# A four-layer forward pass on one core: norm and residual in turn on DVE, latent products operand by operand, decays by ACT's bias

## The chip, the cores and the metric

One core of a Trainium2 chip runs the whole program. TensorE (PE) multiplies into PSUM, VectorE (DVE), ScalarE (ACT) and GpSimd (POOL) do the rest, and SyncE (SP) and ACT issue DMAs. The metric is device time of one execution in microseconds (us), the median of three runs.

## What is computed

The input is 1024 tokens of 1024 numbers, float32. Three layers follow each other, retention with gated output, latent attention (MLA) and gated linear attention (GLA), then a feed-forward network with squared ReLU and a last norm (the reference also defines forgetting attention, which its depth of one leaves out). The parts that matter here, cut from the reference:

```python
def rmsnorm(x, g):
    y = xf * lax.rsqrt(jnp.mean(xf * xf, axis=-1, keepdims=True) + RMS_EPS)
    return (y * g.astype(jnp.float32)).astype(x.dtype)
# end of the retention layer and of the MLA layer
return x + rmsnorm(y, g_post)
# start of the second layer
a = rmsnorm(h, g_kv) @ w_kv_a              # latent keys and values, 256 + 64 wide
proj = rmsnorm(h, g_pre) @ w_in            # latent queries, 384 wide, and the gate
# GLA, one chunk: b is the running sum of the log decays
k_dec = kb * jnp.exp(b_last - b)
decay = jnp.exp(jnp.where(causal, b_i - b_j, -jnp.inf))
```

## The kernel before

Activations lie transposed: eight tiles (k = 0 to 7) of 128 features by 512 tokens for each half h of the tokens. Each operand of a product is split in a high part (ACT copies) and a low part (DVE subtracts), and each product takes three matmuls (`mm3`, lines 227 to 232). Weights are split likewise (`load_parts`, line 128): SP loads them, POOL scales them by a gain where there is one (L135), ACT writes the high part (L143), DVE the low part (L144); two raw buffers, four slots for the parts. PSUM has eight banks in three pools; `acc_tile` hands out five of them in turn.

Norms: `Norm.add` squares a tile on ACT and adds it up on the engines of its list in turn (L265); `rstd` sums over partitions on PE (L273), makes mean plus epsilon on DVE (`var`, L309) and the power on POOL (L312); `spread` brings the result to all partitions by PE (L320) and ACT (L328). `Next` takes each finished tile of a layer: it squares it, stores it, splits it into operands (L187, L188) and, some due units later, emits the norm (`rows`). `tick` counts these units down as products are emitted. `Later` counts them down on demand, when something asks for a value that has not been emitted yet.

First hand-over. `a_last` (L1062) does the last quarter of the first layer's output product for both halves and adds it to y (L1085). After each half, `finish(h)` (L1144) multiplies all y tiles by gain and norm on DVE (L1152), adds the layer's input `xres` (L1161, tile 0 on DVE, the others on POOL) and gives the tile to `nb`, whose norm alternates between DVE and POOL. Then `gemm_group` (L348) makes the latent products in groups of three weights: queries (h = 0), keys and values (h = 0), queries (h = 1), keys and values (h = 1). Each product runs through all eight operands before the next begins, and the three are evacuated at the end with the new norm (`raw`, L1221, `rope`, L334 to L340). The gate products follow.

Second hand-over. `b_out` (L1517) makes the second layer's output product in four parts (`ps_out`), adds them (L1546), and defers `finished` (L765), which multiplies by gain and norm (L778) and adds the layer's input (L782, on DVE for the tiles in `B_ADDS`, on POOL otherwise). `each` is the third layer's `NextC`: its `Blocks` split the tiles and make seven sums of blocks for a multiplication scheme with seven products per 2 by 2 blocks (L193, L454, L463). The first three weight jobs (`job_of_c`, L1852) begin on the first blocks; their weights' low parts are on POOL.

Levels. In the third layer `c_levels` (L1687) makes the masked decays of one head and half, eight times: the decayed key `kd` (POOL subtracts, ACT exponentiates L1706, POOL multiplies L1707, PE transposes L1772), and seven levels of blocks of width L = 64 to 1: `decayed` subtracts a reference column on DVE (L1725), takes the magnitude and the exponential on ACT (L1726, L1727), and multiplies on DVE (L1730). It runs as a side generator between the layer's products.

The order on each engine is not the program's: a planner places every instruction by priority and by times from its own model of the machine, when the program is built. `high_priority` and `urgent` raise a step. On the chip each engine then runs its list in order, and an instruction that waits holds up all behind it.

## Time and profile before

| | us |
|---|---|
| median of 3 runs | 2600.33 |
| lowest, highest | 2598.05, 2600.61 |
| the profiled execution | 2598.72 |
| its span, first to last instruction | 2596.7 |
| PE busy in it | 2448.0 |
| DVE busy | 2001.0 |
| POOL busy | 1184.9 |
| ACT busy | 1114.1 |

The span is what the trace covers; 2.0 us of the execution lie around it. Times in the trace count from the span's start. L12 is line 12 of the kernel. A releaser in brackets is what ended an engine's idle time. A granted clock of 1.00 is 2.4 GHz, 0.50 is 1.2 GHz. In a time line an instruction's length holds some overlap with the next one, so the pitch between starts is the cost of one in a row.

### The profile page before, as it was taken

The page shows a single profiled execution, that of the slowest core. Times are in us where ns is not written, and L with a number is a line of the kernel's source. Part 1 is how long each engine was busy: PE and PEld are TensorE (multiplying, and loading weights), DVE is VectorE, ACT ScalarE, POOL GpSimd, SP SyncE. Part 2 cuts the span into 40 slices and gives each one's busy share as a digit, 9 for nine tenths or more (in the row PEclk, how much of TensorE's full clock was granted, in tenths as well). Part 3 has the DMA queues.
Part 4 walks back from the last instruction along what each step waited for, and adds up shares of the span by engine and source line. Part 5 has one row for each costly group of instructions (what it writes and reads, how often), then busy time and mean ns, then how long its engine had stood idle before and what let it go on. Part 6 is the DMA issues. An engine that isn't in the chain of part 4 may idle for free.

```text
span 2596.7 us, 35526 instructions
## 1 busy us (share of the span) xinstructions
PE 2448.0 (94%) x12676; PEld 2049.2 (79%) x12676; DVE 2001.0 (77%) x2939; ACT 1114.1 (43%) x1932; POOL 1184.9 (46%) x873
## 2 busy tenths in 40 slices
PE   7999999999998899999998998899999999999998
PEld 5888888878786688888887787877777888788877
DVE  8787686789987853766659768895788777867786
ACT  7323323254443333555544354444453333543334
POOL 4344454534754831322206344554546666433355
PEclk8999999999998899999999899999999999999999
DMA  6523223534333322122234242456424344644432
GB/s 230 158 84 122 102 82 121 207 98 126 108 116 98 122 87 78 51 67 78 86 116 142 79 134 102 155 174 207 134 106 154 138 155 152 236 141 140 142 130 90
DMA packets 153101, 327.62 MB, mean 126 GB/s; under 512 B 17467, under 2 KB 20923, under 8 KB 152924
## 3 DMA queue, kind: packets, MB, share of 16 engines
q1 hardware_dynamic: 131036, 285.49, 33.6%
q10 hardware_dynamic: 21888, 39.86, 4.0%
q8 instruction: 100, 1.64, 0.3%
q14 instruction: 77, 0.63, 0.1%
HBM read 224.09 MB, written 99.09 MB: 124 GB/s over the span
## 4 chain that ended last, share of the span: by engine, by line
PE 64%; DVE 20%; issue 5%; DMA 4%; POOL 3%; ACT 3%; SPq 0%; ACTq 0%; DVEq 0%; POOLq 0%
PE ps L230 13%; PE ps L232 13%; PE ps L231 13%; DVE wl L630 3%; DVE swap L840 2%; PE ps L522 2%; PE ps L521 2%; PE ps L523 1%; DVE z L1730 1%; PE ps_g L230 1%; PE ps_g L232 1%; PE ps_g L231 1%; PE pt L1453 1%; DVE y L550 1%; PE ps_out L230 1%
## 5 line engine op out<-in xcount | busy, mean ns | idle before, releaser
L629 ACT ACTIVATE wh<-ws 128x1024 fp32r<-128x1024 f32 (+3 forms) x200 | 142.7, 725 | 193.3 <-PE ps L231 109.4
L630 DVE TENSOR_TENSOR wl<-ws,wh 128x1024 fp32r<-128x1024 f32 (+3 forms) x196 | 205.0, 1053 | 20.1 <-ACT wh L629 19.6
L638 POOL TENSOR_TENSOR wsb<-wsc 128x512 f32<-128x512 f32 (+2 forms) x72 | 102.7, 1426 | 254.2 <-issue 173.2
L230 PE MATMUL ps<-hi,wh 128*128 128x512 f32 (+1 forms) x488 | 185.9, 382 | 2.5 <-DVE y L2174 1.7
L232 PE MATMUL ps<-hi,wl 128*128 128x512 f32 (+1 forms) x488 | 184.0, 382 | 3.9 <-DVE wl L630 3.0
L231 PE MATMUL ps<-lo,wh 128*128 128x512 f32 (+1 forms) x488 | 185.4, 380 | 0.0
L629 ACT ACTIVATE wh<-wsb 128x1024 fp32r<-128x1024 f32 (+2 forms) x76 | 73.6, 968 | 222.1 <-PE ps L231 165.1
L638 POOL TENSOR_TENSOR ws<-ws,wsb 128x512 f32<-128x512 f32 (+2 forms) x72 | 99.1, 1377 | 116.9 <-DVE wl L630 116.9
L1428 POOL TENSOR_SCALAR p<-p,rl 128x512 f32<-128x512 f32 (+2 forms) x96 | 61.0, 646 | 195.8 <-DVE rl L1426 94.0
L638 POOL TENSOR_TENSOR wsb<-ws,wsb 128x512 f32<-128x512 f32 (+2 forms) x72 | 114.0, 1583 | 75.5 <-DMA ws<-w_a 40.9
L550 DVE TENSOR_TENSOR y<-ps,y 128x512 f32<-128x512 f32 x112 | 76.6, 684 | 75.5 <-PE ps L232 45.0
L550 DVE TENSOR_TENSOR one<-ps,one 128x512 f32<-128x512 f32 x168 | 113.9, 681 | 19.4 <-PE ps L232 17.3
L550 DVE TENSOR_TENSOR y<-ps,one 128x512 f32<-128x512 f32 x108 | 73.5, 685 | 64.0 <-ACT one L556 23.0
L630 DVE TENSOR_TENSOR wl<-wsc,wh 128x1024 fp32r<-128x1024 f32 (+2 forms) x76 | 108.0, 1425 | 11.2 <-ACT wh L629 10.6
L232 PEld LDWEIGHTS ps<-hi,wl 128*128 128x128 f32 x488 | 91.7, 188 | 25.6 <-DVE wl L630 5.2
L638 POOL TENSOR_TENSOR wsc<-wsc,ws 128x512 f32<-128x512 f32 (+2 forms) x72 | 110.9, 1540 | 0.0
L230 PEld LDWEIGHTS ps<-hi,wh 128*128 128x128 f32 x488 | 91.7, 188 | 23.3 <-DVE y L2174 2.3
L2174 DVE TENSOR_TENSOR y<-ps,y 128x512 f32<-128x512 f32 x124 | 83.3, 681 | 30.3 <-PE ps L232 29.9
L231 PEld LDWEIGHTS ps<-lo,wh 128*128 128x128 f32 x488 | 91.7, 188 | 18.8
L630 DVE TENSOR_TENSOR wl<-wsb,wh 128x1024 fp32r<-128x1024 f32 (+2 forms) x76 | 96.7, 1273 | 12.7 <-ACT wh L629 12.3
L188 DVE TENSOR_TENSOR lo<-lo,hi 128x512 fp32r<-128x512 f32 x106 | 78.3, 767 | 25.2 <-ACT hi L187 25.2
L629 ACT ACTIVATE wh<-wsc 128x1024 fp32r<-128x1024 f32 (+2 forms) x76 | 73.2, 968 | 57.2 <-PE ps L231 38.4
(473 smaller groups left out, 8594.5 us busy)
## 6 DMA issues: line engine op xcount, KB each, us to landing
lo<-u SPq DMA_DIRECT2D x98, 256.0 KB, 5.2
ws<-w_ff SPq DMA_DIRECT2D x23, 512.0 KB, 3.7
ws<-w_a SPq DMA_DIRECT2D x21, 512.0 KB, 4.9
u<-y SPq DMA_DIRECT2D x42, 256.0 KB, 2.1
ws<-w_b SPq DMA_DIRECT2D x20, 512.0 KB, 3.4
wsc<-w_a SPq DMA_DIRECT2D x16, 512.0 KB, 4.2
v<-v SPq DMA_DIRECT2D x32, 256.0 KB, 3.2
gate<-g SPq DMA_DIRECT2D x32, 256.0 KB, 3.3
```

The source lines that it names most:

```text
L188: (lo_eng or nc.vector).tensor_tensor(out=lo, in0=src, in1=hi.bitcast(F32), op=ALU.subtract)
L230: nc.tensor.matmul(ps, lh, rh, start=start, stop=False)
L231: nc.tensor.matmul(ps, lh, rl, start=False, stop=False)
L232: nc.tensor.matmul(ps, ll, rh, start=False, stop=stop)
L521: nc.tensor.matmul(o, xh[:, ts], wh[:, c], start=k == 0, stop=False)
L522: nc.tensor.matmul(o, xh[:, ts], wl[:, c], start=False, stop=False)
L550: nc.vector.tensor_tensor(out=o, in0=p, in1=i, op=ALU.add)
L629: nc.scalar.activation(out=hi, in_=raw, func=AF.Copy)
L630: lo_eng.tensor_tensor(out=lo, in0=raw, in1=hi.bitcast(F32), op=ALU.subtract)
L638: eng.tensor_tensor(out=o, in0=x, in1=y, op=op)
L1428: nc.gpsimd.tensor_scalar(out=pr, in0=pr, scalar1=rl, scalar2=0.0, op0=ALU.mult, op1=ALU.add)
L2174: nc.vector.tensor_tensor(out=t, in0=ps, in1=t, op=ALU.add)
```

## The change

At both hand-overs, DVE now does the multiplication and the residual addition of a tile one after the other, through two turn buffers, for all eight tiles; POOL does none of these additions. The residual loads of the first hand-over are issued in `a_last`, after the first of its four weights. The norm sums of `nb` are all on POOL, its due time is 13 instead of 10 units. `gemm_group` runs through the operands in its outer loop: for each of the eight, the three matmuls of all three products, with its ticks in two portions. The order of the groups is queries (h = 0), keys and values (both halves), queries (h = 1), so the key and value weights are loaded once and the query weights twice, nine loads for twelve. In the levels, `kd` is made by four exponentials of 128 columns, each with its reference column as ACT's bias, and a product on DVE; for L = 64 and 32 the magnitude is taken by ACT from b with the reference column as bias, in four pieces of 128 and eight of 64 columns, without the subtraction. The low parts of the first weights of the third layer are on DVE.

```diff
-B_ADDS = ((0, 4), (0, 1, 2, 3))
+LEVEL_ACT = 32
-B_WAIT = 10
+B_WAIT = 13
 def gemm_group(srcs, xs, wide, evac, halves=(0, 1), **kw):
...
-            acc = []
-            for m, w in enumerate(ws):
-                acc.append(acc_tile("ps_grp", wide))
-                gemm_t(acc[m], w, 0, [xs[k, h] for k in range(NK)])
+            acc = [acc_tile("ps_grp", wide) for _ in ws]
+            for k in range(NK):
+                c = slice(k * P, k * P + P)
+                for ps, (wh, wl) in zip(acc, ws):
+                    mm3(ps, wh[:, c], wl[:, c], *xs[k, h], k == 0, k == NK - 1)
+                if k % 4 == 3:
+                    tick(len(ws))
...
 class Next:
-        def __init__(self, name, g=None, wait=TILE_UNITS):
+        def __init__(self, name, g=None, wait=TILE_UNITS, on=(nc.vector, nc.gpsimd)):
...
-                self.norm[h] = Norm(D)
+                self.norm[h] = Norm(D, self.on)
...
 def finished(y, h, norm, post, latest, each, order):
...
-            for k in order:
-                t = y[k, h]
+            turns = [stage("turn") for _ in range(2)]
+            for i, k in enumerate(order):
+                t, u = y[k, h], turns[i % 2]
                 nc.vector.scalar_tensor_tensor(
-                    out=t, in0=t, scalar=gain(post, k), in1=rb, op0=ALU.mult, op1=ALU.mult
+                    out=u, in0=t, scalar=gain(post, k), in1=rb, op0=ALU.mult, op1=ALU.mult
                 )
-                eng = nc.vector if k in on_vector else nc.gpsimd
-                eng.tensor_tensor(out=t, in0=t, in1=old[k], op=ALU.add)
+                nc.vector.tensor_tensor(out=t, in0=u, in1=old[k], op=ALU.add)
...
 def a_last(g, norms):
...
                 for s in range(4):
+                    if s == 1:
+                        for k in range(NK):
+                            xres[k, h] = slots.get("xres")
+                            load(xres[k, h], a["x"][k, h])
...
-        nb = Next("b", wait=B_WAIT)
+        nb = Next("b", wait=B_WAIT, on=(nc.gpsimd,))
         def finish(h):
...
+            turns = [slots.get("turn") for _ in range(2)]
             for k in range(NK):
-                xs = slots.get("xres")
-                load(xs, a["x"][k, h])
+                xs = xres.pop((k, h))
...
-                    out=y[k, h],
+                    out=t,
...
-                eng = nc.gpsimd if k else nc.vector
-                eng.tensor_tensor(out=y[k, h], in0=y[k, h], in1=xs, op=ALU.add)
+                nc.vector.tensor_tensor(out=y[k, h], in0=t, in1=xs, op=ALU.add)
...
-        for h in range(2):
-            for o, evac, g in ((0, lat_q.add, gq), (3, evac_kv, gk)):
-                gemm_group(
...
+        for o, evac, g, hs in (
+            (0, lat_q.add, gq, (0,)), (3, evac_kv, gk, (0, 1)), (0, lat_q.add, gq, (1,))
+        ):
+            srcs = [a["w_b"][o + m] for m in range(3)]
+            gemm_group(srcs, nb.x, True, evac, hs, scale=g, nk=NK)
...
 def c_levels(i, h):
...
-        nc.gpsimd.tensor_tensor(
-            out=chunks(kd),
-            in0=chunks(b)[:, :, P - 1 : P].to_broadcast([P, 4, P]),
-            in1=chunks(b),
-            op=ALU.subtract,
-        )
-        nc.scalar.activation(out=kd, in_=kd, func=AF.Exp)
-        nc.gpsimd.tensor_tensor(out=kd, in0=kd, in1=k, op=ALU.mult)
+        for c in range(4):
+            cs = slice(c * P, (c + 1) * P)
+            nc.scalar.activation(
+                out=kd[:, cs],
+                in_=b[:, cs],
+                func=AF.Exp,
+                scale=-1.0,
+                bias=b[:, cs.stop - 1 : cs.stop],
+            )
+        nc.vector.tensor_tensor(out=kd, in0=kd, in1=k, op=ALU.mult)
...
-            nc.vector.tensor_tensor(out=zv, in0=bv, in1=ref, op=ALU.subtract)
-            nc.scalar.activation(out=z, in_=z, func=AF.Abs)
+            if L >= LEVEL_ACT:
+                for o in range(0, HALF, 2 * L):
+                    nc.scalar.activation(
+                        out=z[:, o : o + 2 * L],
+                        in_=b[:, o : o + 2 * L],
+                        func=AF.Abs,
+                        scale=-1.0,
+                        bias=b[:, o + L - 1 : o + L],
+                    )
+            else:
+                nc.vector.tensor_tensor(out=zv, in0=bv, in1=ref, op=ALU.subtract)
+                nc.scalar.activation(out=z, in_=z, func=AF.Abs)
...
 def job_of_c(n, early=False, bank=bank5):
-            w.first(nc.gpsimd if n < C_BEGIN else nc.vector)
+            w.first()
```

## Rows read from the trace of the kernel before

**Rows 1.** The page, parts 1 and 2: busy time by engine, PE's granted clock in 40 slices.

```profile
PE 2448.0 (94%) x12676; PEld 2049.2 (79%) x12676; DVE 2001.0 (77%) x2939; ACT 1114.1 (43%) x1932; POOL 1184.9 (46%) x873
...
PEclk8999999999998899999999899999999999999999
```

**Rows 2.** Table by stage: from:to, length, busy PE PEld DVE ACT POOL (instructions), clock, DMA share, GB/s.

```profile
812.90:918.50 105.60, 82.63 (x370) 66.18 (x370) 89.84 (x87) 42.26 (x64) 75.73 (x42) 0.87 0.37 122
817.50:831.10 13.60, 8.14 (x16) 4.87 (x16) 13.60 (x16) 7.36 (x13) 5.99 (x4) 0.50 0.67 225
918.50:1016.00 97.50, 97.50 (x436) 78.91 (x436) 38.26 (x48) 25.16 (x38) 14.40 (x8) 1.00 0.27 91
1360.20:1469.00 108.80, 95.61 (x462) 80.41 (x461) 92.48 (x106) 49.07 (x78) 57.83 (x34) 0.87 0.34 111
1435.30:1452.30 17.00, 14.93 (x47) 12.80 (x48) 17.00 (x27) 8.96 (x15) 7.09 (x5) 0.50 0.24 82
1495.00:1755.00 260.00, 232.19 (x1542) 205.74 (x1541) 218.00 (x345) 132.76 (x214) 127.78 (x92) 0.97 0.43 141
```

**Rows 3.** PE's time line: start, length, engine, line, out<-in, [idle before, releaser].

```profile
786.28 0.39 PE L232 MATMUL ps<-uh,wl 128*128 128x512 f32 x1
786.51 0.39 PE L230 MATMUL ps<-uh,wh 128*128 128x512 f32 x1
...
819.19 1.89 PE L230 MATMUL ps_grp<-xh,wh 128*128 128x512 f32 x3 [6.29 <-ACT xh L187]
...
872.14 0.79 PE L230 MATMUL ps_grp<-xh,wh 128*128 128x512 f32 x1 [12.65 <-DVE raw L1221]
```

**Rows 4.** DVE's and POOL's time lines, the first layer's end, first half.

```profile
805.16 11.13 DVE L1152 SCALAR_TENSOR_TENSOR y<-y,gains,rbp 128x512 f32<-128x512 f32 x8
...
808.96 11.82 POOL L1161 TENSOR_TENSOR y<-y,xres 128x512 f32<-128x512 f32 x7
```

**Rows 5.** DVE's time line: the norm's variance, and the evacuation that uses it.

```profile
848.03 0.16 DVE L309 TENSOR_SCALAR var<-ps_stat 128x4 f32<-128x4 f32 x1
...
871.40 1.87 DVE L1221 TENSOR_TENSOR raw<-ps_grp,rb 128x512 f32<-128x512 f32 x3
```

**Rows 6.** DVE by line and shape, 805 to 918: count, busy, mean ns, idle before.

```profile
L1234 DVE SCALAR_TENSOR_TENSOR raw<-raw,gains,rbp 128x512 f32<-128x512 f32 x3 | 2.1, 747 | 1.1 <-ACT rbp L328 1.1
...
L188 DVE TENSOR_TENSOR ql<-raw,qh 128x512 fp32r<-128x512 f32 x3 | 2.0, 683 | 0.0
```

**Rows 7.** Time lines of ACT and DVE: the two parts of one weight.

```profile
794.20 1.06 ACT L143 ACTIVATE wh<-ws 128x1024 fp32r<-128x1024 f32 x1 [1.25 <-PE ps L231]
...
795.30 1.22 DVE L144 TENSOR_TENSOR wl<-ws,wh 128x1024 fp32r<-128x1024 f32 x1 [0.23 <-ACT wh L143]
```

**Rows 8.** Waits (us, times, longest), groups by shape and DVE's time line, 1350 to 1470.

```profile
PE ps_stat L273 <- DVE acc L265: 6.5, 1, 6.5
...
L778 DVE SCALAR_TENSOR_TENSOR by<-by,gains,rbp 128x512 f32<-128x512 f32 x16 | 19.1, 1261 | 1.9 <-ACT rbp L328 1.7
...
L630 POOL TENSOR_TENSOR wl<-ws,wh 128x1024 fp32r<-128x1024 f32 x4 | 10.6, 2641 | 4.0 <-ACT wh L629 4.0
...
1457.67 0.68 DVE L188 TENSOR_TENSOR x4l<-by,x4h 128x512 fp32r<-128x512 f32 x1
```

**Rows 9.** Waits and groups by shape, 1495 to 1755; ACT's short forms from the whole span.

```profile
PE ps_kd L1772 <- POOL kd L1707: 9.9, 5, 4.2
...
L1707 POOL TENSOR_TENSOR kd<-kd,k 128x512 f32<-128x512 f32 x8 | 13.3, 1663 | 0.7 <-ACT kd L1706 0.7
...
L1725 DVE TENSOR_TENSOR z<-b 128x512 f32<-128x512 f32 x56 | 53.0, 966 | 16.3 <-DMA b<-cb 12.4 <-DMA ckt<-kd 4.0
...
L1726 ACT ACTIVATE z<-z 128x512 f32<-128x512 f32 x56 | 34.5, 626 | 59.4 <-DVE z L1725 59.0
...
L629 ACT ACTIVATE wh<-ws 128x256 fp32r<-128x256 f32 x20 | 8.3, 413 | 15.9 <-POOL ws L638 13.5 <-PE ps L231 2.4
...
L1414 ACT ACTIVATE p<-S,nm 128x128 f32<-128x128 f32 x16 | 5.8, 364 | 11.3 <-PE pt L1453 10.0 <-DVE ql L1306 1.3
```

More of the change, by code (lines that the diff above doesn't have):

```diff
@@ L360, in tile_kernel @@
     class Next:
-        def __init__(self, name, g=None, wait=TILE_UNITS):
-            self.name, self.g, self.wait = name, g, wait
+        def __init__(self, name, g=None, wait=TILE_UNITS, on=(nc.vector, nc.gpsimd)):
+            self.name, self.g, self.wait, self.on = name, g, wait, on
             self.x, self.dram, self.norm = Later(), {}, {}
@@ L747, in __init__ @@
         def __init__(self, name, g=None, wait=TILE_UNITS, norms="NN", on=(nc.gpsimd,), prefer=()):
-            super().__init__(name, g, wait)
+            super().__init__(name, g, wait, on)
             self.x7 = Blocks(slots, 4, prefer)
-            self.norms, self.on = norms, on
+            self.norms = norms
         def take(self, k, h, t):
@@ L763, in tile, with finished @@
             return stage(name) if name == "sq" else super().tile(name)
-    def finished(y, h, norm, post, latest, each, order, on_vector):
+    def finished(y, h, norm, post, latest, each, order):
         old = {k: slots.get("res") for k in range(NK)}
@@ L1058, in a_turn @@
                 yield
-        og = {}
+        og, xres = {}, {}
         def a_last(g, norms):
@@ L1146, in finish @@
             rb = spread(r4, pc, "rbp")
+            turns = [slots.get("turn") for _ in range(2)]
             for k in range(NK):
-                xs = slots.get("xres")
-                load(xs, a["x"][k, h])
+                xs = xres.pop((k, h))
                 hurry = tc.high_priority() if h == 0 and A_HURRY else ExitStack()
                 hurry.__enter__()
+                t = turns[k % 2]
                 nc.vector.scalar_tensor_tensor(
-                    out=y[k, h],
+                    out=t,
                     in0=y[k, h],
@@ L1164, in finish @@
                 hurry.__exit__(None, None, None)
+            slots.put(*turns)
         slots.held.update(NORM_TAGS)
@@ L1264, in evac_kv @@
             defer(keep(h, kr))
-        for h in range(2):
-            for o, evac, g in ((0, lat_q.add, gq), (3, evac_kv, gk)):
-                gemm_group(
-                    [a["w_b"][o + m] for m in range(3)],
-                    nb.x,
-                    True,
-                    evac,
-                    (h,),
-                    scale=g,
-                    nk=NK,
-                )
+        for o, evac, g, hs in (
[3 more added lines that the diff above has]
+            gemm_group(srcs, nb.x, True, evac, hs, scale=g, nk=NK)
         for m in range(8):
@@ L1552, in b_out @@
                 old = lambda k, h: nb.dram[k, h]
-                defer(finished(y, h, norm, "g_post_b", old, each, B_ORDER[h], B_ADDS[h]))
+                defer(finished(y, h, norm, "g_post_b", old, each, B_ORDER[h]))
     W2 = a["w_out_c"]
@@ L1699, in c_levels @@
         kd = stage("kd")
-        nc.gpsimd.tensor_tensor(
-            out=chunks(kd),
-            in0=chunks(b)[:, :, P - 1 : P].to_broadcast([P, 4, P]),
-            in1=chunks(b),
-            op=ALU.subtract,
-        )
-        nc.scalar.activation(out=kd, in_=kd, func=AF.Exp)
-        nc.gpsimd.tensor_tensor(out=kd, in0=kd, in1=k, op=ALU.mult)
+        for c in range(4):
[8 more added lines that the diff above has]
+        nc.vector.tensor_tensor(out=kd, in0=kd, in1=k, op=ALU.mult)
         nc.gpsimd.tensor_tensor(out=qe, in0=qe, in1=q, op=ALU.mult)
```

## The prediction

> **What bounds the kernel now.** I read the page first: TensorE (PE) is busy for 94% of the span, and its granted clock is full in nearly all slices [rows 1]. The time can therefore only fall where PE idles, or where it runs at the lower of its two levels (1.2 instead of 2.4 GHz). Next I read the table by stage [rows 2]. In the stretch where the first layer hands over to the second (812.9 to 918.5 us) PE works for 82.63 of 105.6 us. That is 23.0 us idle, and in the spell 817.5 to 831.1 the clock is 0.50 while PE is busy for 8.14 us, which costs another 4.1 us. So 27 us can be won there. In the stretch from the second layer's end into the third (1360.2 to 1469) PE works 95.61 of 108.8 us: 13.2 us idle. The mean clock of 0.87 means some 28 us at the lower level; in 17 of them, 1435.3 to 1452.3, PE is busy for 14.93 us and loses 7.5. The rest I put at 3, so some 24 us can be won. In the third layer's level stage (1495 to 1755) PE idles for 27.8 of 260 us. Behind each hand-over stands work that PE alone sets: from 918.5 to 1016 it is busy throughout, with DVE at 38 of 97.5 us. What is won ahead of it is kept.
>
> Then PE's time line and waits say who ends the idle time. At 819.19 PE starts the latent products after 6.29 us of waiting for the first operand (xh, made by ACT from DVE's sum). At 872.14 it starts again after 12.65 us, released by DVE's evacuation `raw` [rows 3]. DVE's and POOL's lines say why [rows 4]: at 805.16 DVE does all eight norm multiplications in one block of 11.13 us, while POOL does seven residual additions in 11.82 us. The first tile is added behind DVE's block, although the products read the tiles in order 0 to 7. The second wait is the norm chain of the next input: its `var` is at 848.03, but the evacuation that needs its result is at 871.40 [rows 5], queued on DVE, ACT and POOL behind the second half's block. PE has five accumulators there. Three hold the first group's products and two the next group's, so PE stops.
>
> **The change, part by part.**
>
> Alternating on DVE (first hand-over). An undisturbed DVE instruction takes 0.75 us (scalar_tensor_tensor) or 0.68 us (tensor_tensor), a weight's low part 1.22 us [rows 6, 7]. Beside POOL the eight multiplications took 11.13/8 = 1.39 us each. After the change, the first tile is ready 0.75 + 0.68 us into the block, so at 805.2 + 1.4, and with ACT's split at about 808.5. PE comes free at 812.9, so the wait of 6.29 us goes, and the spell at half clock behind it.
>
> What is late next is the last operand of the second half. I sum DVE's work up to it from 805.2: 16 multiplications (12.0), 16 additions and 16 low parts (32 at 0.68: 21.9), four weights' low parts (4.9), and three evacuations, four norm sums, five evacuations of the latent groups and five pieces of the rope, 17 at 0.68 (11.6): 50.4 us. To it comes what POOL takes from DVE. POOL no longer adds residuals but does all 14 norm sums of the new input, and I count six scalings and powers beside them: 20 instructions. In the block of [rows 4] eight multiplications took 11.13 - 8 x 0.75 = 5.1 us too long while about five POOL additions ran: 1.0 us for each. DVE also has PSUM reads and waits between, so I take 0.7: 14 us. The last operand stands at 805.2 + 50.4 + 14 = 870.
>
> Products operand by operand. Three accumulators grow together, so PE can use each operand as it arrives: nine matmuls, 9 x 0.23 = 2.1 us [rows 3]. Before, the third product's start and not the last operand set the time. The stretch has four groups of 72 products. With the last operand at 870, group three ends at about 872 and group four 72 x 0.23 = 16.6 us later, with some 2 us of norm sums: 891 instead of 918.5. This says 27, all there is. Against it stand two new waits. A group now opens three accumulators at once, so its third product waits for the evacuation of the group before, hence for that norm chain; and weights are kept in four slots, three of which now fall free together, so two weights of the next group are split only after a group's end (1.06 us ACT and 1.22 us DVE each [rows 7], about 4 us). Matmuls of the products that do have bank and weights can run in the meantime if the planner puts them there. I charge 5 us. **This hand-over: -22 us.** Ends: -27 (all of it), and -9 if POOL blocks DVE longer.
>
> The Trainium skill ("SBUF — State Buffer", section "SBUF: two separate sides") says that GpSimd and a DVE instruction with two SBUF inputs exclude each other for a whole instruction. By it each of the 20 POOL instructions would cost DVE up to 1.69 us (11.82/7 [rows 4]) and the last operand would stand near 889; the row shows 1.0 us.
>
> Three weights are loaded once instead of twice, which saves three DMAs, three scalings on POOL and three splits, off the path. Residual loads are issued earlier on SP, ahead of some weights; the weights of the last output product hide them. If a slot is not free there, one weight comes late, at most about the 6.29 us already seen. The later due time of the norm sum costs nothing: it is emitted on demand when the evacuation asks for it.
>
> Alternating on DVE (second hand-over). Here the multiplications took 1.26 us on average, 16 of them [rows 8], 8.2 us over their own time. DVE gains ten additions (6.8 us) and the four low parts of the first weights that POOL made in 2.64 us each (4 x 1.22 = 4.9). So 11.7 us come, 8.2 go there and some more at DVE's other instructions, since POOL's ten additions and four low parts vanish: DVE's load stays as it is, within 4 us. What changes is the order: PE waits 6.5 us at the norm sum for DVE's `acc`, behind evacuations that stood in DVE's queue behind the first half's block, and the second half's block begins only after it. Its last operand is ready at 1457.67 + 0.68, and PE ends its products 11 us later, half of it backlog from the lower clock. DVE idles for 16 us of this stretch (108.8 - 92.48), part of it around the two blocks, which can go, and with its norm sum on time PE has finished the first products when the operands come. I take the last operand 5 us earlier and the backlog 5 us shorter: **-10 us.** Ends: -24 (all) and +4 (DVE's load up, order worth nothing).
>
> Key decay and wide blocks (third layer, eight blocks). PE waits 9.9 us for the decayed key from POOL [rows 9]. Two POOL instructions (the product alone 1.66 us) and one exponential become four short exponentials with a bias and a product on DVE of 0.68 to 0.97 us; I count 6 of the 9.9 us as won. DVE loses 16 subtractions and gains eight products at 0.97: -7.7 us, half of it on the path: -4. ACT pays: a 512-column instruction takes 626 ns, one of 256 columns 413, so 0.83 ns per column; 128 columns with a bias took 364, and 64 would take about 311 (estimate from these). So 4 x 0.364 + 4 x 0.364 + 8 x 0.311 - 3 x 0.626 = 3.5 us per block, 28 us in all. ACT is busy for 132.8 of 260 us in this stage [rows 2], which is the cover; I charge 2 us. **-8 us.** Ends: -18, and +15 if ACT's pieces lie on the path.
>
> The Trainium skill ("VectorE: DVE Perf Modes", section "The TRN2 errata — SBUF-src ops pay a fixed extra latency per instruction") speaks against this part: it wants tiles of 512 elements or more, since each instruction pays its latency again. The trace agrees, with about 0.2 us of 413 ns not going into columns; whether it decides is the third rival's question.
>
> Sum: -22 - 10 - 8 = -40. The profiled execution took 2598.7 us (span 2596.7 and 2.0 around it), so 2558.7. The median shown is 2600.33, 1.6 above it: **2560 us.**
>
> **The rivals.**
>
> 1. DVE stays the bound at both hand-overs: POOL's sums block it longer, and the additions it has taken over fill what the order frees. For it: DVE is busy for 89.84 of 105.6 and 92.48 of 108.8 us. Against it: PE's operand order lets it follow DVE. First hand-over -9, second 0, levels -5: 2586.
>
> 2. The planner places the blocks as before (all multiplications, then the additions), since it orders by its own durations. Then the first operand comes no earlier, the change does not do what it says at the hand-overs, and the levels' gain is eaten by the added work: 2598.
>
> 3. ACT decides in the levels: 28 us of short instructions stand in its queue ahead of weights' high parts and evacuations. Levels +13 instead of -8: 2581. For it: ACT's order is fixed, and an instruction that waits for its tile holds up all behind it. Against it: half its time is free.
>
> 4. Slower: feeding PE operand by operand holds it at the lower clock. For it: from 1435.3 to 1452.3 PE was fed in just this way, busy for 14.93 of 17.0 us, and the clock was 0.50 [rows 2]. At that level a group takes 2 x 16.6 = 33 us. It decides when the operands of the whole latent stretch come more slowly than one in 2.1 us: three groups, and about 9 us for the 370 - 288 = 82 small matmuls beside them (estimate, half a product's pitch), then end at 812.9 + 99 + 9 = 921, the fourth at 938, 20 us later than now. Nothing is won in the second hand-over, where the same happens now, and the levels give -8: 2612. Against it: the tiles of the first half are made while PE still works on the output product.
>
> **How the numbers follow.** Chances: forecast 0.58 (2543 to 2577), rival 1 0.17, rival 2 0.07, rival 3 0.08, rival 4 0.10. Faster by over 0.2% (5 us, about what a measurement of this kernel tells from no change): 0.58 + 0.17 + 0.08 = 0.83; within it 0.07; slower 0.10. The range takes in the forecast and rivals 1 and 3: 2540 to 2590. The low end is all of the first hand-over (-27), -18 and -15.
>
> **What would show it.** Right: DVE's line alternates the two instructions from about 805 on; PE has no wait over 3 us between 812 and 880 and ends the latent products near 895; its second hand-over ends near 1437 on the new scale (10 us more won); the wait of PE for `kd` is below 4 us. Wrong: a wait of PE for `raw` or for a weight's low part at a group's start (rivals 1 and 4), a granted clock of 0.50 over most of the latent groups (4), a residual addition that still follows the whole block (2), PE or DVE waiting for ACT's Abs pieces (3).

## The result: 2580 us, half of the gain that was forecast

| | us | ratio to before (95%) |
|---|---|---|
| before, median of 4 runs beside it | 2599.86 | |
| after, median of 4 (2572.77 to 2580.43) | 2579.94 | 0.9919 (0.9903 to 0.9935) |
| its profiled execution | 2580.32 | |
| forecast | 2560 (2540 to 2590) | |

The change gains 20 us. The forecast said 40. The time lies in the range, and near the 2581 of the third rival, but not for that rival's reason, as will be seen.

The page of after, parts 1 and 2, as [rows 1]:

```profile
PE 2457.3 (95%) x12676; PEld 2058.8 (80%) x12676; DVE 1978.9 (77%) x2948; ACT 1130.4 (44%) x2033; POOL 1122.5 (44%) x834
...
PEclk8999999999998999999999999999999999999999
```

PE is the bound as before. Its busy time has grown by 9 us at the same count; a matmul at the lower level counts for longer (0.79 us in the time line below, 0.39 in [rows 3]). So the question is where idle time and lower level went. The table by stage of after, as [rows 2] (from:to, length, busy time of PE, PEld, DVE, ACT, POOL with instructions, clock, DMA share, GB/s):

```profile
811.60:910.20 98.60, 84.98 (x378) 68.36 (x377) 83.84 (x93) 35.21 (x57) 58.24 (x34) 0.90 0.25 91
...
819.30:836.30 17.00, 11.68 (x33) 8.62 (x34) 16.04 (x18) 4.49 (x8) 10.31 (x6) 0.60 0.25 93
...
860.20:867.10 6.90, 4.71 (x11) 3.75 (x12) 6.90 (x9) 3.14 (x5) 2.27 (x2) 0.51 0.10 38
867.10:910.20 43.10, 43.10 (x215) 35.91 (x215) 34.69 (x41) 15.47 (x25) 28.39 (x17) 1.00 0.25 86
...
1378.90:1452.60 73.70, 67.63 (x353) 58.03 (x353) 65.85 (x96) 32.84 (x52) 19.52 (x15) 0.86 0.28 95
...
1452.60:1913.80 461.20, 428.91 (x2410) 362.28 (x2409) 347.88 (x537) 246.29 (x511) 206.17 (x148) 0.95 0.44 146
```

The latent products (first row) still hold 13.6 us without work. PE's and DVE's time lines there (start, length, engine, line, out<-in, idle before and its releaser), as [rows 3, 4]:

```profile
811.62 0.85 PE L230 MATMUL ps_grp<-xh,wh 128*128 128x512 f32 x3
813.50 0.50 PE L231 MATMUL ps_grp<-xl,wh 128*128 128x512 f32 x1 [1.03 <-DVE xl L188]
...
820.41 0.79 PE L232 MATMUL ps_grp<-xh,wl 128*128 128x512 f32 x1 [4.08 <-DVE wl L144]
...
862.38 0.80 PE L230 MATMUL ps_grp<-xh,wh 128*128 128x512 f32 x1 [4.31 <-DVE raw L1229]
```

```profile
804.43 1.40 DVE L1160 SCALAR_TENSOR_TENSOR turn<-y,gains,rbp 128x512 f32<-128x512 f32 x2
805.75 0.68 DVE L1168 TENSOR_TENSOR y<-turn,xres 128x512 f32<-128x512 f32 x1
...
813.97 0.68 DVE L1092 TENSOR_TENSOR one<-ps,one 128x512 f32<-128x512 f32 x1
814.58 0.68 DVE L265 TENSOR_TENSOR acc<-acc,sq 128x512 f32<-128x512 f32 x1
...
818.08 2.28 DVE L144 TENSOR_TENSOR wl<-ws,wh 128x1024 fp32r<-128x1024 f32 x1
...
842.25 0.75 DVE L1160 SCALAR_TENSOR_TENSOR turn<-one,gains,rbp 128x512 f32<-128x512 f32 x1 [5.40 <-ACT rbp L328]
...
870.22 1.78 DVE L188 TENSOR_TENSOR xl<-y,xh 128x512 fp32r<-128x512 f32 x1
...
878.33 0.69 DVE L334 TENSOR_TENSOR rope<-ps_grp,cr 128x512 f32<-128x512 f32 x1 [1.84 <-POOL cr L1268]
```

The block of eight multiplications is gone, and so is the wait of 6.29 us for the first operand. The one wait of 12.65 us has become two of 4.08 and 4.31 and several short ones. The last operand is there at 870.2 + 1.8 = 872. In before it was there at 875.7, 3.7 us later; PE's start on the products, on the first operand, has moved by 7.6 (819.19 in [rows 3], 811.62):

```profile
875.00 0.68 DVE L188 TENSOR_TENSOR xl<-y,xh 128x512 fp32r<-128x512 f32 x1
```

To compare kernels, the traces are cut at the first or last matmul on a tile. Times count from the start of the first layer's output product (758.2 in before, 757.0 in after), so that what differs ahead of it is left out. "Third layer" runs from the products of its low part (`ps_low`) to the end of its output product. "Order" names the order of ScalarE's instructions in the third layer's levels, compared instruction by instruction: kernels with one letter have the same list.

| kernel | median us | ratio (95%) | end of latent products | end of 2nd layer's products | from there to low part | third layer | order |
|---|---|---|---|---|---|---|---|
| before | 2600 | | 160.3 | 632.9 | 81.1 | 459.7 | B |
| after | 2579.9 | 0.9919 (0.9903 to 0.9935) | 153.2 | 621.8 | 73.7 | 461.2 | A |
| e1 | 2588.4 | 0.9957 (0.9945 to 0.9969) | 153.3 | 622.2 | 73.7 | 473.6 | own |
| e2 | 2580.5 | 0.9928 (0.9900 to 0.9957) | 152.0 | 620.9 | 73.7 | 462.5 | own |
| e3 | 2580.2 | 0.9926 (0.9903 to 0.9949) | 160.6 | 630.9 | 75.0 | 452.4 | C |
| e4 | 2580.4 | 0.9929 (0.9909 to 0.9949) | 154.0 | 622.7 | 79.9 | 455.1 | C |
| e5 | 2575.1 | 0.9906 (0.9890 to 0.9923) | 153.5 | 622.3 | 79.2 | 455.4 | C |
| e6 | 2577.4 | 0.9914 (0.9895 to 0.9933) | 154.9 | 626.8 | 75.1 | 449.8 | C |
| e7 | 2590.1 | 0.9960 (0.9946 to 0.9974) | 162.3 | 636.9 | 78.5 | 452.5 | C |
| e8 | 2584.8 | 0.9941 (0.9926 to 0.9956) | 150.3 | 623.9 | 72.1 | 463.9 | A |
| e9 | 2573.2 | 0.9891 (0.9872 to 0.9911) | 152.0 | 620.3 | 74.5 | 450.1 | C |
| e10 | 2570.6 | 0.9882 (0.9861 to 0.9903) | 148.0 | 616.9 | 76.3 | 454.0 | C |
| e11 | 2586.0 | 0.9949 (0.9932 to 0.9965) | 153.3 | 621.6 | 76.1 | 462.5 | B |
| e12 | 2578.1 | 0.9916 (0.9896 to 0.9937) | 153.4 | 622.0 | 82.6 | 452.3 | C |

Each row's parts come from one execution, and executions of one kernel differ by up to 9 us from their median; the profiled one of e9 was the fastest of its five (2566.5), that of e5 the slowest of its four (2580.1). So the columns tell where, the medians how much. Over the eight kernels with order C the profiled executions lie 0.3 us above their medians on average, so their mean can be used.

### The profile page after: what moved, and what is told of

Same layout as the page of the kernel before. It is cut to its first block, busy times and chain, and to the rows that moved or that the text cites. A ratio compares the mean times of both kernels' runs of the same rounds, so it can differ in the third digit from the quotient of the medians.

```text
span 2578.5 us, 35600 instructions
## 1 busy us (share of the span) xinstructions
PE 2457.3 (95%) x12676; PEld 2058.8 (80%) x12676; DVE 1978.9 (77%) x2948; ACT 1130.4 (44%) x2033; POOL 1122.5 (44%) x834
## 5 line engine op out<-in xcount | busy, mean ns | idle before, releaser
L633 DVE TENSOR_TENSOR wl<-ws,wh 128x1024 fp32r<-128x1024 f32 (+3 forms) x200 | 211.2, 1063 | 24.7 <-ACT wh L632 23.7
L553 DVE TENSOR_TENSOR y<-ps,one 128x512 f32<-128x512 f32 x108 | 73.7, 686 | 71.6 <-PE ps L232 27.8
L553 DVE TENSOR_TENSOR one<-ps,one 128x512 f32<-128x512 f32 x168 | 114.1, 682 | 12.7 <-PE ps L232 11.6
```

The lines of the kernel that those rows point to most:

```text
L553: nc.vector.tensor_tensor(out=o, in0=p, in1=i, op=ALU.add)
L633: lo_eng.tensor_tensor(out=lo, in0=raw, in1=hi.bitcast(F32), op=ALU.subtract)
```

## The experiments

**First question: which part of the change brings the 20 us?** Compared with before, the end of the latent products had moved by 7 us and the low part by 18 on the table's scale, but the third layer took as long as before, in spite of its edits. Four kernels take one part back each.

e1, both level edits back (the score blocks' edit alone is `LEVEL_ACT = 128`):

```diff
-LEVEL_ACT = 32
+LEVEL_ACT = 128
-        for c in range(4):
...
-        nc.vector.tensor_tensor(out=kd, in0=kd, in1=k, op=ALU.mult)
+        nc.gpsimd.tensor_tensor(
+            out=chunks(kd),
...
+        nc.scalar.activation(out=kd, in_=kd, func=AF.Exp)
+        nc.gpsimd.tensor_tensor(out=kd, in0=kd, in1=k, op=ALU.mult)
```

> The changed kernel with both edits of the level blocks taken back: key decay on GpSimd and ScalarE, and all seven score blocks by a VectorE subtraction. Theory L (the blocks of the levels are a serial chain that sets the end of that stage, and ScalarE's short pieces with a bias lie on it whole): eight blocks again stand 24.9 us apart in place of 28.2, so the time falls by 7 x 3.3 = 23 us, to 2557 (2552 to 2563). Theory E (something else sets the stage's end, for example the layer's products or the last stores; the longer interval is only slack that is used up): 2580, within 4 us of the changed kernel. Theory K (the level edits do win what they were meant to, and the loss comes from the earlier arrival of the stage): 2588 or more.

Measured 2588.4: 8 us slower than after, in the range of theory K. Theory L, that ScalarE's short pieces cost the stage its gain, has fallen: without them the stage is longer (473.6). How much of that is e1's own order can't be told from this run.

e2, only the score blocks back:

```diff
-LEVEL_ACT = 32
+LEVEL_ACT = 128
```

> The changed kernel with only the wide score blocks taken back to VectorE; the key decay stays with ScalarE's four biased pieces and VectorE's product. Of the 3.5 us that ScalarE pays more per block, 4 x 388 + 8 x 335 ns less two wide pieces of 626 ns = 3.0 us are the score blocks' and 0.5 us the key decay's. Theory L with ScalarE's sum as the price: 8 x 3.0 = 24 us less than the changed kernel, about 2557 to 2560, and at most 4 us from the run with both edits back. Theory K2 (the key decay's product, now queued on VectorE, is what makes the block longer): 2575 or more here, and the gain appears only where the key decay is back on GpSimd. Theory E: 2580.

Measured 2580.5, as after. By itself this says that the score blocks are worth nothing, but e2 has a list order of its own, so edit and order can't be told apart here.

e3, the first hand-over back (`finish` with POOL's additions, `gemm_group` product by product, old order of groups, residual loads in `finish`, `nb` on two engines):

```diff
-B_WAIT = 13
+B_WAIT = 10
-                nc.vector.tensor_tensor(out=y[k, h], in0=t, in1=xs, op=ALU.add)
+                eng = nc.gpsimd if k else nc.vector
+                eng.tensor_tensor(out=y[k, h], in0=y[k, h], in1=xs, op=ALU.add)
...
```

> The changed kernel with the whole first hand-over taken back (residual adds on GpSimd, two-engine norm sums, latent products one by one, the order of the groups). If the shift of 8.3 us that the two traces show at the end of the latent products reaches the end: 2588 (2585 to 2592). If the level blocks swallow it (they end when their own chain ends, whatever comes before): 2580. If the gain was worth the forecast 22 us and was lost later: 2600.

e4, the second hand-over back:

```diff
-                nc.vector.tensor_tensor(out=t, in0=u, in1=old[k], op=ALU.add)
+                eng = nc.vector if k in on_vector else nc.gpsimd
+                eng.tensor_tensor(out=t, in0=t, in1=old[k], op=ALU.add)
-            w.first()
+            w.first(nc.gpsimd if n < C_BEGIN else nc.vector)
```

> The changed kernel with the second hand-over taken back (adds divided between VectorE and GpSimd, first weights of the third layer split on GpSimd). The two traces show 10 to 11 us won between the end of the first hand-over's work and the low part of the third layer. If all of it reaches the end: 2590 (2587 to 2594). If the chain of level blocks hides it: 2580. If the return of the weights to GpSimd slows the level blocks too: above 2594.

Measured 2580.2 and 2580.4: either hand-over can be taken back, and the time stays. That is the outcome foreseen for "the level blocks swallow it". But the table shows something else: both kernels reach the third layer 7 to 10 us later, and then take 452.4 and 455.1 us for it, after 461.2. The same code got faster. Set side by side, ScalarE's list of the levels is the same in e3 and e4, and agrees with that of after in about two thirds of its instructions (0.66, matched in their order); VectorE's lists differ as well. ScalarE's part where a weight's high part stands earlier or later among the decays. So there were two theories: the third layer ends when it ends, whatever comes before (S), or the planner, to which the hand-overs look shorter, has put the third layer into a worse order (P).

**Second question: is it the order?** e5 and e6 take back small things that bring the order of e3 and e4; e7 has that order with a late start; e8 keeps the order of after.

e5:

```diff
-            w.first()
+            w.first(nc.gpsimd if n < C_BEGIN else nc.vector)
```

> The changed kernel with one thing taken back: the low parts of the third layer's first weights are on GpSimd again. With it the planner places the whole level stage in the order that it has in e3 and e4 (ScalarE's list there is the same, instruction for instruction), where the changed kernel has another. Theory P (the hand-overs' gain is lost because the planner gave the third layer a worse order, by 6 to 9 us): the stretch from the low part to the third layer's output product takes 452 to 456 us in place of 461, and the time falls to 2572 (2568 to 2577) although nothing is made faster. Theory S (that stretch ends when its own chain ends, whatever comes before): 2580. If the weights on GpSimd cost their 4 x 1.4 us: 2586.

e6:

```diff
-        for o, evac, g, hs in ((0, lat_q.add, gq, (0,)), (3, evac_kv, gk, (0, 1)), (0, lat_q.add, gq, (1,))):
+        for h in range(2):
+            for o, evac, g in ((0, lat_q.add, gq), (3, evac_kv, gk)):
```

> The changed kernel with the four latent groups in the old order (queries, keys and values, queries, keys and values), so that the key and value weights are loaded twice. It too gets the level order of e3 and e4. Theory P: the third layer's stretch takes 452 to 456 us; the time is 2572 plus what the order of the groups is worth, 0 to 4 us: 2570 to 2578. Theory S: 2580.

e7, the kernel before with the two level edits alone (the diff of e1 the other way round):

> The kernel before with the level edits alone (key decay and wide blocks), both hand-overs as before. Its level stage has the order of e3 and e4. Theory P: the third layer begins where it does before (1472) and its stretch takes 452 to 456 us in place of 459.7: 4 to 8 us less than before, 2593 (2591 to 2597). Theory S: the stretch ends at 1913 as in the changed kernel, e3 and e4, so 2580. If the level edits are worth what taking them back from the changed kernel cost (8 us in time, 12 in the stretch): 2588 to 2592.

e7 settles theory S: 2590.1 and not 2580. Starting at 1471.4, its third layer takes 452.5 us, so what is won or lost ahead of it does count. The 452.5 are in the range of theory P, the time is faster than its 2593 (2591 to 2597) and in that of the third outcome (2588 to 2592). e5 (2575.1) and e6 (2577.4) have lower medians than after although each takes a gain back; their intervals overlap with that of after.

e6 shows one thing more. With the old order of the groups the second layer's products end at 626.8, and at 620.3 to 622.7 in the eight kernels that have the whole new first hand-over. So some 5 us of this hand-over's gain, in one execution, hang on the order of the groups and the three weight loads that it saves, which the working put "off the path".

e8, the latent products one by one:

```diff
-            for k in range(NK):
-                for ps, (wh, wl) in zip(acc, ws):
-                    mm3(ps, wh[:, c], wl[:, c], *xs[k, h], k == 0, k == NK - 1)
+            for m, w in enumerate(ws):
+                gemm_t(acc[m], w, 0, [xs[k, h] for k in range(NK)])
```

> The changed kernel with the latent products one by one again (each through all eight operands), all else kept; the level stage keeps the changed kernel's order. In the changed kernel TensorE is starved between 816 and 836: VectorE finishes an operand every 4.0 us, and the group's nine products of one take 2.1. Theory O (working operand by operand is what hides part of that): the second and third product of the first group, 48 x 0.23 = 11 us, come behind the last operand in place of 3 or so, so the latent products end 8 us later, at 918, and the time is 2588. Theory C (the short waits at the lower clock cost as much as the early work gains): the latent products end at 910 within 3 us, and the time is 2580.

Measured 2584.8, between the theories, with an interval that overlaps with that of after. In the trace the latent products end earlier (150.3 for 153.2), but other small matmuls have moved behind them, and the gate products begin at 153.6 for 153.0; the second layer's products end 2.1 us later. So the order operand by operand is worth between nothing and 5 us, and its gain does not show in the stretch for which it was made. The third layer takes 463.9, the length of after, whose order it has.

e9, a third turn buffer at the second hand-over, which leaves the work as it is and brings order C:

```diff
-            turns = [stage("turn") for _ in range(2)]
+            turns = [stage("turn") for _ in range(3)]
-                t, u = y[k, h], turns[i % 2]
+                t, u = y[k, h], turns[i % 3]
```

> The changed kernel with three turn buffers in place of two at the second hand-over, and nothing else. The buffers do not matter there for the time, but with three the planner places the third layer's level stage in the order of e3 to e7. Theory P (the order cost the changed kernel 6 to 9 us): the stretch from the low part to the third layer's output product takes 450 to 456 us in place of 461, the rest as in the changed kernel: 2571 (2568 to 2575). Theory S (the order is not it; e5 and e6 were faster for what they took back): 2580.

e11, e9 with the old levels (order B):

> e9 with both level edits taken back. Its level stage has the order of the kernel before. Theory P, by which the parts add up when the order is not disturbed: from the end of the second layer's products to the third layer's output product it takes 534 us (before: 540.8, less 7 for the second hand-over), and the level edits are worth 10 us, as e7 showed against the kernel before: 2581 (2578 to 2584). Theory L (the level edits are worth more behind early hand-overs, as the change against e1 seemed to show): 2588 or more.

Third layer of e9, e11 and e7, columns as above, each in its own trace:

```profile
1450.20:1900.30 450.10, 421.83 (x2408) 356.67 (x2407) 347.41 (x537) 246.64 (x511) 198.57 (x148) 0.96 0.45 149
```

```profile
1455.50:1918.00 462.50, 420.38 (x2408) 354.21 (x2407) 362.12 (x545) 226.67 (x407) 219.48 (x164) 0.97 0.44 145
```

```profile
1471.40:1923.90 452.50, 424.14 (x2406) 358.87 (x2405) 347.87 (x537) 246.60 (x511) 197.80 (x147) 0.96 0.45 148
```

e9: 2573.2, as theory P said, 6.7 us under after by the medians, while the intervals still overlap by a little. The hand-over where the buffer stands did not get shorter (74.5 for 73.7); the third layer did. Eight kernels with order C take 449.8 to 455.4 us for it, the two with order A 461.2 and 463.9. Theory P has held: the order costs the change about 7 us by the medians, 8 to 10 by these stretches. PE's waits in the third layer (total, times, longest), after first and then e9 and e11:

```profile
PE ps_lv L1766 <- DVE z L1744: 10.5, 6, 3.1
PE ps_kd L1786 <- DVE kd L1711: 9.3, 4, 4.0
```

```profile
PE ps_lv L1766 <- DVE z L1744: 5.7, 8, 1.9
PE ps_kd L1786 <- DVE kd L1711: 4.4, 1, 4.4
```

```profile
PE ps_kd L1784 <- POOL kd L1709: 9.7, 5, 4.4
PE ps_lv L1764 <- DVE z L1742: 9.4, 12, 1.6
```

In order A the decayed key comes late 4 times, for 9.3 us in after and 9.5 in e8; in the eight kernels with order C once or twice, for 4.4 to 6.0. The wait for `z` is 10.5 and 11.2 us in order A, 4.4 to 5.7 in order C. These waits make up only part of it. Of the 11.1 us between after and e9, PE's idle time is 4.0 (32.3 less 28.3, as other waits have grown), and the other 7.1 are PE busy for longer with the same matmuls (428.9 for 421.8), more of them at the lower level (0.95 for 0.96 of the clock).

e11 came out between its theories (2581 and 2588): 12.7 us slower than e9, with intervals apart. e7 gave 10.6 against before. This is the levels' worth as far as it can be told, since the old levels bring an order of their own (B). Why the planner's own times tip over just when both hand-overs are short was not found out; any one of four small edits (e5, e6, e9, e12) tips them back.

**Third question: why is the first hand-over worth less than forecast?** e10 is e9 with the norm sums of `nb` on PE, in place of 14 additions on POOL:

```diff
-                self.norm[h] = Norm(D, self.on)
+                self.norm[h] = NormOnTensor(D) if self.name == "b" else Norm(D, self.on)
```

> e9, and the norm sums of the first hand-over are made by TensorE (four small matmuls of each squared tile with a column of ones) in place of 14 additions on GpSimd. Theory D (GpSimd's additions beside VectorE hold it up by 0.7 us each, and VectorE's pace of 4.0 us per operand starves TensorE): the pace falls by 14 x 0.7 / 16 = 0.6 us per operand, the latent products end 5 to 10 us earlier than in e9, and the time is 2564 (2560 to 2568). Theory F (VectorE's own instructions set the pace, the small matmuls cost what GpSimd gives back): within 3 us of e9.

Latent products of e9 and of e10 (columns as above), then two groups of DVE (count, busy us, mean ns, idle before) and PE's waits, after first, e10 second:

```profile
810.00:907.40 97.40, 83.94 (x378) 67.55 (x377) 84.11 (x93) 35.08 (x56) 57.62 (x34) 0.93 0.27 92
```

```profile
814.40:906.20 91.80, 91.43 (x475) 77.24 (x475) 65.88 (x92) 35.56 (x57) 39.96 (x21) 0.96 0.28 95
```

```profile
L188 DVE TENSOR_TENSOR xl<-y,xh 128x512 fp32r<-128x512 f32 x12 | 13.2, 1110 | 1.0 <-ACT xh L187 1.0
...
L1168 DVE TENSOR_TENSOR y<-turn,xres 128x512 f32<-128x512 f32 x12 | 11.0, 913 | 0.0
...
PE ps_grp L230 <- DVE raw L1229: 4.3, 1, 4.3
PE ps_grp L232 <- DVE wl L144: 4.1, 1, 4.1
PE ps_grp L231 <- DVE xl L188: 3.9, 3, 1.8
```

```profile
L1168 DVE TENSOR_TENSOR y<-turn,xres 128x512 f32<-128x512 f32 x12 | 8.1, 683 | 0.0
L188 DVE TENSOR_TENSOR xl<-y,xh 128x512 fp32r<-128x512 f32 x12 | 8.1, 685 | 1.0 <-ACT xh L187 1.0
...
PE ps_grp L231 <- DVE xl L188: 0.4, 1, 0.4
```

The waits of PE go with POOL's sums, those for a weight's low part and for `raw` too, which the working had put down to slots and banks: 13.5 us idle (e9) become 0.4. PE also has 97 more small matmuls (475 for 378) that can fill a wait; what is free of this is DVE's own line. DVE's additions take 683 ns instead of 913, its low parts 685 instead of 1110. The last operand is ready at 858.4, 13.6 us before that of after (14.2 before that of e9 on the table's scale), so each of the 14 sums had cost 1.0 us, as [rows 4] said. PE pays 7.5 us more busy time for the small matmuls, so the latent products end 4 us earlier than in e9 and the second layer's products 3.4. The median is 2.6 us under that of e9 (2570.6), with overlapping intervals, so the time alone is that of theory F; DVE's line is that of theory D, whose 5 to 10 us and 2564 did not come, for what PE pays. Against after the median is 9 us lower, with intervals that just touch. It is the lowest median here.

**Fourth question: what carries the second hand-over?** e12 is the counterpart of e5, with the low parts on DVE and the additions on POOL:

```diff
-                nc.vector.tensor_tensor(out=t, in0=u, in1=old[k], op=ALU.add)
+                eng = nc.vector if k in on_vector else nc.gpsimd
+                eng.tensor_tensor(out=t, in0=t, in1=old[k], op=ALU.add)
```

> The changed kernel with the other part of the second hand-over taken back: the ten residual additions are on GpSimd again and there are no turn buffers, but the low parts of the first weights stay on VectorE (the opposite of e5). The level stage has the order of e3 to e9, so e9 is what it is compared with. From the end of the second layer's products to the third layer's output product e9 takes 524.6 us, e4 and e5 535.0 and 534.6. Theory W (the low parts alone carry the second hand-over's gain; the alternation of multiplication and addition is worth nothing by itself): 525 to 528 us, time 2573 to 2576. Theory A (the alternation is needed as well): 532 to 536 us, time 2580 to 2584.

From the end of the second layer's products to that of the third layer's output product e12 takes 82.6 + 452.3 = 535 us, as theory A said, though the time of 2578.1 lies between the two. The stretch up to the low part in e5 and e12, with PE's wait for the norm sum and DVE's multiplications, after's next to last; the last row is the same stretch of before:

```profile
1378.60:1457.80 79.20, 69.93 (x356) 59.54 (x357) 69.04 (x94) 34.10 (x54) 25.45 (x19) 0.85 0.26 90
...
PE ps_stat L273 <- DVE acc L265: 4.0, 1, 4.0
...
L782 DVE SCALAR_TENSOR_TENSOR turn<-by,gains,rbp 128x512 f32<-128x512 f32 x8 | 7.7, 1006 | 0.3 <-ACT rbp L328 0.3
```

```profile
1379.10:1461.70 82.60, 72.03 (x356) 61.77 (x357) 66.89 (x92) 34.11 (x54) 30.97 (x21) 0.83 0.24 83
...
PE ps_stat L274 <- DVE acc L266: 5.0, 1, 5.0
...
L782 DVE SCALAR_TENSOR_TENSOR by<-by,gains,rbp 128x512 f32<-128x512 f32 x8 | 9.5, 1259 | 2.0 <-ACT rbp L329 2.0
```

```profile
PE ps_stat L273 <- DVE acc L265: 0.6, 1, 0.6
...
L782 DVE SCALAR_TENSOR_TENSOR turn<-by,gains,rbp 128x512 f32<-128x512 f32 x8 | 6.7, 870 | 4.7 <-ACT rbp L328 4.7
```

```profile
1391.00:1472.20 81.20, 70.29 (x358) 60.36 (x357) 65.93 (x86) 32.83 (x52) 38.40 (x25) 0.83 0.25 85
```

POOL is busy for 19.5 us of this stretch in after, 25.5 in e5, 31.0 in e12, 38.4 in before. With it grow DVE's multiplication (870, 1006, 1259 ns; 1261 in [rows 8]) and the wait for `acc` (0.6, 4.0, 5.0; 6.5 in [rows 8]). So neither the alternation nor the low parts carry the gain by themselves; it needs both. That it is POOL's quiet beside DVE which brings it fits these rows, but was not tried by itself, and beyond 25 us of POOL the stretch does not grow steadily: e7 has 78.5 us, with POOL busy for 36.8.

## Why the prediction was half right

| part | forecast | found |
|---|---|---|
| first hand-over | -22 | about -12 in the traces; -7 by the medians of e9 and e3 |
| second hand-over | -10 | about -6 in the traces; -7 by e9 and e4 |
| levels | -8 | about -8 in the traces; -10.6 by e7, -12.7 by e9 and e11 |
| order of the third layer | not foreseen | +7 (after against e9) |
| sum | -40 | -20 |

The values from the traces are differences of the table's means: 633.6 less 621.7 at the end of the second layer's products (before, e3 and e7 against the eight kernels with the whole new first hand-over), 80.3 less 74.5 for the way from there to the low part (before, e4, e5, e7 and e12 against the others), and 461.1 (order B) less 452.7 (order C). They add up to -26; by the medians the intervals of e3 and e4 overlap with that of e9. e9, which has all three and order C, is 27.5 us faster than the runs of before beside it (2600.76). That the time lies in the range is luck in part: the range was widened for rivals 1 and 3, and the order, which no step held, took 7 us of it.

**First hand-over: the start and the last operand were right, what lay between was not.** DVE alternates from 804, the first wait is gone, and the last operand came at 872 (forecast 870). The step that failed is the next one: "group three ends at about 872". It needs PE to have worked off all before. At 872 there were not 19 us of work left, as the step says, but 38 (to 910.2). PE had been idle for 13.6 us, where the working charged 5 for all new waits, and had spent 20.5 us at 1.2 GHz (mean clock 0.60 from 819.3 to 836.3, 0.51 from 860.2 to 867.1), for which nothing was charged. In those spells it was busy for 14.3 us (11.68 and 4.71, less 2.1 at the full clock from 826.1 to 829.5) with work that takes half at 2.4 GHz, so 7 us more. 13.6 + 7 - 5 is 16 too little, which leaves -6 of the -22; 8.3 were found at the end of the latent products in the traces' own times, 7.1 on the table's scale, and the rest of the -12 behind it (see e6). DVE takes 4.2 us per operand (67.6 for 16) and the first group has 2.1 us of products for each. The working's own numbers give 4.0 and 2.1; it named this comparison as the condition of rival 4, and did not charge it in the forecast. The "no wait over 3 us between 812 and 880" was wrong twice, and both waits, for a weight's low part and for `raw`, are of the kinds that were named as signs of rivals 1 and 4. Rival 1 put -9 on this hand-over, closer than the forecast; rival 4 had the mechanism of the lower clock, which came in spells and not over the whole stretch.

The price of POOL beside DVE was mis-sized too: 0.7 us per instruction was taken, 1.0 read in [rows 4], and 1.0 found by e10. The operand's time came out right nevertheless, by errors that cancel. DVE's own work was put too high: up to 872 it does none of the five pieces of the rope (the first is at 878.33) and only three of the five evacuations of the latent groups, and its instructions in a row stand 0.60 us apart and not 0.68 (813.97 to 814.58). 16 multiplications at 0.66, 42 instructions at 0.60 and five low parts at 1.14 are 41.5 us, where the working had 50.4. Idle time of DVE was put at nothing and is 6.4 us, 5.40 of them for the second half's norm. Of the 67.6 us from 804.4 to 872, 19.7 are left, 1.0 for each of the 20 POOL instructions that start in them. The Trainium skill ("SBUF — State Buffer", section "SBUF: two separate sides") has GpSimd and a DVE instruction with two SBUF inputs lock each other out for the whole instruction, which would be up to 1.76 us, the mean of one sum in after. The trace goes the rule's way, by 1.0 of the 1.76.

**Second hand-over: right in kind, and nearer than it looked.** DVE's load stayed as it was, as forecast (65.9 us in before and after), and the wait of 6.5 us for `acc` went to 0.6. The backlog after the last operand did not go with it: PE is still at 1.2 GHz for 20.5 us of the 73.7, 27.3 before. The working said that the order does it. e5 keeps the order and loses most of the gain, so the order alone does not; POOL's quiet, the other thing that e5 and e12 take away, is the likelier cause.

**Levels: the sum was right, its terms were not, so that it was right is luck in part.** ACT's price was 28 us in the working and is 20.0 (246.6 less 226.7 in e9 and e11). The groups of after say why:

```profile
L1731 ACT ACTIVATE z<-b 128x64 f32<-128x64 f32 x64 | 16.2, 335 | 0.0
L1731 ACT ACTIVATE z<-b 128x128 f32<-128x128 f32 x32 | 10.2, 388 | 0.0
```

One piece is longer than estimated (335 for 311 ns, 388 for 364), but 64 of them are busy for 16.2 us, 253 ns each in a row: a length holds overlap with the next. DVE gained 14.7 us and not 7.7 (362.1 less 347.4). PE's wait for `kd`, forecast below 4 us, is 4.4 in e9 and was 9.3 in after. Rival 3 (ACT decides) is out: with the pieces the kernel is faster, by 10.6 us (e7 against before) and 12.7 (e9 against e11), and taking them away made it no faster (e2) or slower (e1).

**What no step held** is the fourth line of the table. The prediction knew that a planner orders every engine by its own times, and made a rival of it at the hand-overs (rival 2). That shorter hand-overs could reorder a stage 500 us later, whose code for this is the same, was nowhere.

What stays open: what the score blocks are worth without the key decay, because every kernel that parts them has its own order; whether POOL's quiet alone carries the second hand-over; and why the planner's order tips over.

## What to carry to other kernels

Where a planner orders the program, an edit can change the order far away from itself: after any edit, compare each engine's list in the stages that were not touched, and if one has changed, try a neutral edit that brings the old one back, before judging the edit. When an engine is fed piece by piece, hold the time per piece against the work that each piece allows, and charge the idle time, and the lower clock behind it, to every piece; the time of the last piece says nothing about the work left over. Before POOL is given work beside DVE, price it at DVE: here 14 additions, off every path, made DVE's last operand 13.6 us later.

## What the runs showed of the hardware

- DVE instructions with two SBUF inputs took 913 to 1110 ns on average beside POOL's additions and 683 to 685 without them (after, e10), a weight's low part up to 2.28 us instead of 1.22 [rows 7]. One POOL addition cost DVE 1.0 us.
- Short ACT instructions with a bias column: 335 ns for 64 columns, 388 for 128, so 0.83 ns per column and 282 ns for none; in a row they follow each other every 253 and 319 ns. The Trainium skill ("ScalarE: Activation LUTs", section "What ACT_TABLE_LOAD costs") gives about 280 ns and 0.833 ns per column for an instruction with such a bias, with some 93 ns of overlap between one and the next. The lengths agree with the trace; the overlap is 82 and 69 ns here.
- With a wait of 4.31 us that ends at 862.38, PE is at 1.2 GHz from 860.2 to 867.1 (mean granted clock 0.51), so that the first 4.7 us of work behind it are slow as well.
